# A hybrid encoder layer on one core: idle products on other tiles, the order of the attention heads, and the last blocks of w_down row by row

## The chip, the cores and the metric

The kernel runs on one core of a Trainium2 chip. The metric is the device time of one execution in microseconds (us). The time of the kernel before is the median of its runs; one more execution was taken with the hardware profiler, and all rows of the profile come from it.

## The reference

One layer over 512 tokens of width 1024, all in float32. Two mixers in parallel (a state-space scan and a gated spatial mixer) are merged by gates, then come cross-attention to 256 memory tokens and a SwiGLU feed-forward net. What matters for this change is the part from w_out on:

```
h = h + merged @ w_out
q = rms_norm(h) @ w_q; k = memn @ w_k; v = memn @ w_v            # memn = rms_norm(mem), 256 x 1024
s = einsum('blhd,bmhd->bhlm', q, k) * 256 ** -0.5                # 4 heads of 256
o = einsum('bhlm,bmhd->blhd', softmax(s), v)
h = h + o @ w_xo
n = rms_norm(h)
h = h + (silu(n @ w_gate) * (n @ w_up)) @ w_down                 # 2816 wide
return rms_norm(h)
```

## The kernel before

**Three products for one.** Every float32 operand is split in two, a high part and a low one (`split`, L83: ScalarE casts the high part, VectorE subtracts it). A product of two operands is three matmuls, high by high, high by low, low by high (`mm3`, L393; `product`, L1231, has its own). A matmul has 128 rows, a stationary operand of 128 columns and a moving one of 256 or 512. In the profile the three engines are PE (with PEld for the stationary loads), DVE (VectorE) and ACT (ScalarE).

**Weights.** A plan lists all weight blocks in the order of their use. `next_w` (L366) takes the next one; it also starts loads of later blocks (3 ahead, up to 7 for special ones) and the split of those up to 2 ahead (L99). The raw blocks, high parts and low parts rotate through 3 buffers each (tags raw, hi and lo), so a block's split waits until the block three places before it was used to the end. For w_gate, w_up, w_q and w_down the products are of a form with 7 block products in place of 8 (blocks named 1 to 7), whose operands are sums of blocks; some sums are made by DMA in DRAM (dsum) ahead of time.

**Order.** The program is written as one long sequence, but the order on each engine is made by a planner, which runs a timing model and takes, of what its model has ready, the instruction that stands first in the program. Three things bind it: `tc.keep_in_program_order` (named `in_order`, L94) puts an instruction behind the one before it in the program on its engine; `tc.issue_after(ins)` puts what a block traces on that engine behind `ins`; and `later(n, fn)` (L483) traces `fn` at the first `tick` when enough products have been traced. PSUM has two pools: 5 banks ("mm", by `bank`) and 3 ("aux", by `aux`, L73 and L74).

**Operand offsets.** `APART = (48, 112)` (L116) are offsets, in elements, at which the high and low part of some tiles begin: hn, fn, and the sums of the block products. mn's high and low part both begin at 48. ot_hi and ot_lo begin at 0.

**The idle product.** `long_idle` (L551) is one product of 128 by 512 whose result nobody reads. It takes the first 128 columns of its tile as the stationary operand and 512 columns as the moving one. There are two: behind the transposes of the last row before the feed-forward net, on ot_hi (from `feat_norm(..., behind=ot_hi)`, L1630), and at L1787, inside the first of the ten units of w_gate and w_up, on fn_hi.

**From w_out to the units.** `tokm` (L436) makes a product by token rows: w_out in two halves of 512 columns. Each finished row of 128 tokens is added to h, normalized and turned by 8 transposes into feature layout (`to_feat`, L556, tile ptr). w_k (`feat`, L399, stationary w_k, moving mn, 256 columns) and w_v (`tokm`, stationary mn, moving w_v, 512 columns) follow, then w_q in block products, interleaved with the heads of the attention. `scores(hd)` (L1510) makes 24 score products and the softmax of a head (numbered 0 to 3 in the code), `turn_probs` (L1534) turns its probabilities by 8 transposes (tile ppt) and splits them (p_hi, p_lo), and `values` (L1545) makes 12 products (tile po) and splits them into ot. The order at the end of the attention:

```
    values(0, *pts.pop(0))
    probs2 = scores(2)
    turn(1, probs1)
    probs3 = scores(3)
    values(1, *pts.pop(1))
    later(0.2, lambda: turn(2, probs2, last_mm[0].ins))
```

Then w_xo (tile pt): the first half of its columns in four steps of two feature blocks, all four token rows in each step; the first step needs head 0 of ot only. The second half goes two token rows at a time. The rows are normalized and turned (`ptr`), and the gate and up products of the last columns (tile pf) and ten units (tiles px, pv, pq) follow.

**w_down.** `rows_product` (L1762) makes the products of one chunk of a block for given rows; a block has 6 chunks, of 2 feature blocks each and 1 in the last. `down_product` (L1773) runs over the chunks, both token rows (tiles dx[0] and dx[1], 128 by 512) in each. Block 7 goes onto dx; `onto_h` (L1867) subtracts dx from h on VectorE; block 4, the last, goes onto the same dx. At the end the last two chunks of block 4 are held back: dx[1] is added to h without them, row 2 (dx[0]) is finished with them, and the last row gets them as two products of 256 columns (tile pcut). `finish`, `finish_last` and `write` (L1840 to L1865) sum the squares (ACT), take the root (a power on GpSimd, POOL), scale (DVE and ACT) and write out.

Of the kernel before, what the change touches and what calls it, by code (L numbers as in the profile page):

```python
# [17 lines left out]
P = 128  # L18
D = 1024
T = 512  # L20
NT = T // P
KD = D // P
M = 256
NM = M // P
# [28 lines left out]
def hybrid_layer_kernel(  # L53
# [23 lines left out]
    def bank(name):  # L77
        return pm.tile([P, 512], F32, tag="mm", name=name)
# [314 lines left out]
    def mm3(ps, a, b, start, stop, free=False):  # L393

        for i, (x, y) in enumerate(((0, 0), (0, 1), (1, 0))):
            last_mm[0] = nc.tensor.matmul(ps, a[x], b[y], start=start and i == 0, stop=stop and i == 2,  # L396
                                          skip_group_check=free)
# [38 lines left out]
    def tokm(w, c0, act, nk, evac, ntok=NT, last=2, kpt=2, hook=None, cut=None, t0=0, behind=None, fine=False):  # L436

        toks = range(t0, t0 + ntok)
        ps = {t: bank(f"pt{t - t0}") for t in toks}
        nw = nk // kpt  # L440
        held = []
        full = slice(0, 512)
        for wi in range(nw):
            hi, lo = next_w(w, wi * kpt, kpt, c0, 512)
            held.append((wi, hi, lo))
            if hook is not None and wi == nw - last:
                hook()
            if wi < nw - last:
                todo, held = held, []
                for t in toks:  # L450
                    end = cut is not None and t == ntok - 1 and wi == nw - last - 1
                    tok_block(ps[t], t, todo, act, kpt, full, wi == 0, end)
                    if end:
                        cut(None, ps[t])
                    if fine:
                        tick(1.3)
                if not fine:
                    tick(1.3 * ntok)
        for t in toks:
            if cut is not None and t == ntok - 1:  # L460
                for i in range(2):
                    p = aux("pcut", (P, 256))
                    tok_block(p, t, held, act, kpt, slice(256 * i, 256 * i + 256), True, True)
                    cut(i, p)
            else:
                with nullcontext() if behind is None or t > t0 else tc.issue_after(behind):
                    tok_block(ps[t], t, held, act, kpt, full, nw == last, True)
                evac(t, ps[t])
            tick(1.3 * len(held))
# [13 lines left out]
    def later(n, fn):  # L483

        side["later"].append((side["now"] + n, fn))
# [62 lines left out]
        for i in range(2):  # L548
            nc.vector.scalar_tensor_tensor(dst[:, HALF[i]], src[:, HALF[i]], r, g[:, HALF[i]], ALU.mult, ALU.mult)

    def long_idle(x):  # L551

        p = aux("long")
        in_order(nc.tensor.matmul(p, x[:, 0, 0:P], x[:, 0, :], start=True, stop=True))

    def to_feat(src, hi, lo, tsl, full=None, skip=None, part=(0, 1), behind=None):  # L556

        for q in part:
            ps = aux("ptr", (P, 4, P))
            for j in range(4):  # L560
                k = 4 * q + j
                tr = nc.tensor.transpose(ps[:, j, :], src[:, k * P:(k + 1) * P], ident)  # L562
                row_tr[0] = tr.ins
                if behind is not None:
                    in_order(tr)
            if q != skip:
                turned[:] = split(hi[:, 4 * q:4 * q + 4, tsl], lo[:, 4 * q:4 * q + 4, tsl], ps)
            if full is not None:
                nc.scalar.copy(full[:, 4 * q:4 * q + 4, tsl], ps)
        if behind is not None:  # L570
            long_idle(behind)

    xsp = [None]

# [861 lines left out]
    def add_evac(half, layer, fin, fin0=None):  # L1436

        def f(t, ps):
            nc.vector.tensor_tensor(h[:, t, HALF[half]], h[:, t, HALF[half]], ps, ALU.add)
            sum_sq(hss[:, layer, t, half:half + 1], h[:, t, HALF[half]])  # L1440
            if half == 1:
                fin(t, hss[:, layer, t, :])
            elif fin0 is not None:
                fin0(t)
        return f

    def feat_norm(g, hi, lo, full=None, skip=False, behind=None):

        return lambda t, ss: norm_feat(h[:, t, :], g, hi, lo, slice(t * P, (t + 1) * P), ss, full,
                                       0 if skip and t >= 2 else None, behind if t == NT - 1 else None)  # L1450

    mg = (mg_hi, mg_lo)
    for half in range(2):
        tokm(w_out, half * 512, mg, KD, add_evac(half, 0, feat_norm(g_x, hn_hi, hn_lo, hfull, True)))


    mn = (mn_hi, mn_lo)
# [49 lines left out]
            qs[hd] = (qq[:, 0], qq[:, 1])  # L1507
        split(qs[hd][0][:, :, ts], qs[hd][1][:, :, ts], src)

    def scores(hd):  # L1510
        q_hi, q_lo = qs.pop(hd)
        scale = XD ** -0.5
        prob = ap_.tile([P, NT, M], F32, tag="prob", name="prob", bufs=1) if hd % 2 == 0 else \
            np_.tile([P, NT, M], F32, tag="gain", name="prob", bufs=2)
        for i in range(2):
            ps = bank("psc").rearrange("p (t m) -> p t m", t=2)
            for tt in range(2):
                t = 2 * i + tt
                tsl = slice(t * P, (t + 1) * P)
                for k in range(2):  # L1520
                    mm3(ps[:, tt, :], (q_hi[:, k, tsl], q_lo[:, k, tsl]),
                        (kt_hi[:, 2 * hd + k, :], kt_lo[:, 2 * hd + k, :]), k == 0, k == 1)
            mx, nm, sm, rs = (ap_.tile([P, 2], F32, tag=k, name=k, bufs=4) for k in ("mx", "nm", "sm", "rs"))
            nc.vector.tensor_reduce(mx, ps, AX.X, ALU.max)
            nc.vector.tensor_scalar(nm, mx, -scale, None, ALU.mult)
            for tt in range(2):
                nc.scalar.activation(prob[:, 2 * i + tt, :], ps[:, tt, :], AF.Exp, bias=nm[:, tt:tt + 1],
                                     scale=scale, accum_out=sm[:, tt:tt + 1])
            nc.vector.reciprocal(rs, sm)
            for tt in range(2):  # L1530
                nc.vector.tensor_scalar(prob[:, 2 * i + tt, :], prob[:, 2 * i + tt, :], rs[:, tt:tt + 1], None, ALU.mult)
        return prob

    def turn_probs(hd, prob, behind=None):  # L1534
        p_hi = ap_.tile([P, NM, T], F32R, tag="p_hi", name="p_hi", bufs=2)
        p_lo = ap_.tile([P, NM, T], F32R, tag="p_lo", name="p_lo", bufs=2)
        for mt in range(NM):
            ps = aux("ppt", (P, NT, P))
            with nullcontext() if behind is None else tc.issue_after(behind):
                for t in range(NT):  # L1540
                    nc.tensor.transpose(ps[:, t, :], prob[:, t, mt * P:(mt + 1) * P], ident)
            split(p_hi[:, mt, :], p_lo[:, mt, :], ps.rearrange("p t m -> p (t m)"))
        return p_hi, p_lo

    def values(hd, p_hi, p_lo):  # L1545
        for dt_ in range(2):
            ps = bank("po")
            cs = slice(hd * XD + dt_ * P, hd * XD + dt_ * P + P)
            for mt in range(NM):
                mm3(ps, (vts[0][:, mt, cs], vts[1][:, mt, cs]), (p_hi[:, mt, :], p_lo[:, mt, :]), mt == 0, mt == NM - 1)  # L1550
            split(ot_hi[:, 2 * hd + dt_, :], ot_lo[:, 2 * hd + dt_, :], ps)

    def query_product(ps, n, q, start=False):
# [51 lines left out]
    values(0, *pts.pop(0))  # L1605
    probs2 = scores(2)
    turn(1, probs1)
    probs3 = scores(3)
    values(1, *pts.pop(1))
    later(0.2, lambda: turn(2, probs2, last_mm[0].ins))  # L1610
    later(0.7, lambda: turn(3, probs3))
    later(1.2, lambda: values(2, *pts.pop(2)))
    later(1.7, lambda: values(3, *pts.pop(3)))
# [13 lines left out]
    full = fp.tile([P, KD, T], F32, tag="full", name="full", bufs=1)  # L1627


    fin = add_evac(1, 1, feat_norm(g_f, fn_hi, fn_lo, full, behind=ot_hi))  # L1630
    held = []
    for t0 in (0, 2):
        ps = {t: bank(f"pt{t - t0}") for t in (t0, t0 + 1)}
# [233 lines left out]
    def onto_h(ps, t0, half, op):  # L1867
        for t in range(2):
            hs = h[:, t0 + t, HALF[half]]
            nc.vector.tensor_tensor(hs, hs, ps[t], op)  # L1870

    dv = [bank(f"dv{t}") for t in range(2)]
    dq = [bank("dq0"), aux("dq1")]
    down_product(dx, 1, True, range(2, CHUNKS))
# [11 lines left out]
    onto_h(dq, 0, 0, ALU.add)  # L1886
    for t in range(2):
        finish(t)
    down_product(dx, 7, False)
    onto_h(dx, 2, 0, ALU.subtract)  # L1890
    for t in range(2, 4):
        first_half(t, 0)

    held = []
    for c in range(CHUNKS):
        ops_ = next_w(w_down, 4, c)
        if c < CHUNKS - 2:
            rows_product(dx, 4, c, ops_, (0, 1), slice(0, 512), False, c == CHUNKS - 3)
        else:
            held.append((c, ops_))  # L1900
    finish_last(None, dx[1])
    for c, ops_ in held:
        rows_product(dx, 4, c, ops_, (0,), slice(0, 512), False, c == CHUNKS - 1)
    nc.vector.tensor_tensor(h[:, 2, HALF[1]], h[:, 2, HALF[1]], dx[0], ALU.add)
    finish(2)
    for i in range(2):
        p = aux("pcut", (P, 256))
        for c, ops_ in held:
            rows_product({1: p}, 4, c, ops_, (1,), slice(256 * i, 256 * i + 256), c == CHUNKS - 2, c == CHUNKS - 1)
        finish_last(i, p)  # L1910
    tick()
    sx.close()
# [32 lines left out]
```

## Time and profile before

| | us |
|---|---|
| median of 3 runs | 872.29 (871.88 to 872.76) |
| the profiled execution | 871.72 |
| its span, first to last instruction | 869.9 |
| PE busy | 856.6 |
| DVE busy | 648.1 |
| ACT busy | 475.0 |
| POOL busy | 106.2 |

A row of the page's groups, of the timeline or of the chain names the engine, the line, the operation and out<-in by the program's tile names. Line 396 is `mm3`, line 1240 `product`, line 85 and 86 the two steps of `split`, line 562 the transposes of `to_feat`, line 1541 those of the probabilities, line 554 the idle product. In the timeline a row has the start, the duration, and in brackets the idle time of the engine before it and what ended that. Matmuls are pipelined: a matmul's duration is longer than the step to the next one. In the chain of waits a row has start, time and what ran, with the count.

### The profile page before, as it was taken

What the parts mean: (1) busy time and instruction counts of PE and PEld (TensorE: products, weight loads), DVE (VectorE), ACT (ScalarE), POOL (GpSimd) and SP (SyncE); (2) the same over time, 40 slices, a digit from 0 to 9 for tenths busy, and PEclk for the clock granted to TensorE, in tenths of its full rate; (3) what the DMA queues carried; (4) which work ended last, traced back from release to release, by engine and by line L of the source; (5) the groups of instructions that cost most, each with busy time, mean ns of one, the idle gap of its engine ahead of it and who ended that gap; (6) DMA issues with size and microseconds to landing.
All of it is one profiled execution on the core that took longest, in us unless ns stands there. A gap on an engine that the chain in (4) does not pass through costs nothing.

```text
span 869.9 us, 14841 instructions
## 1 busy us (share of the span) xinstructions
PE 856.6 (98%) x5893; PEld 762.3 (88%) x5893; DVE 648.1 (75%) x897; ACT 475.0 (55%) x704; POOL 106.2 (12%) x157
## 2 busy tenths in 40 slices
PE   8999999999999999999999999999999999999996
PEld 6788888888789988899899888999999999988875
DVE  5699588968748658679658646867877768899875
ACT  5544874276437534457557444645545455656663
POOL 1001155100611010110010001001111111000000
PEclk8999999999999999999999999999999999999998
DMA  7549279745639586945688153557798886577672
GB/s 244 153 127 258 72 210 237 169 123 170 158 95 246 142 241 197 284 105 167 206 256 219 50 166 98 145 134 179 173 239 207 209 211 153 134 211 226 198 244 89
DMA packets 110119, 155.40 MB, mean 179 GB/s; under 512 B 8969, under 2 KB 77089, under 8 KB 109986
## 3 DMA queue, kind: packets, MB, share of 16 engines
q1 hardware_dynamic: 91746, 128.27, 46.1%
q0 software_dynamic: 18016, 25.66, 18.6%
q8 instruction: 46, 0.75, 0.4%
q10 hardware_dynamic: 288, 0.52, 0.2%
q14 instruction: 23, 0.19, 0.1%
HBM read 148.70 MB, written 37.20 MB: 214 GB/s over the span
## 4 chain that ended last, share of the span: by engine, by line
PE 94%; ACT 2%; DMA 2%; DVE 1%; issue 1%; SPq 0%; POOL 0%; POOLq 0%; ACTq 0%; DVEq 0%
PE pf L396 25%; PE pt L396 18%; PE px L1240 13%; PE dx L396 7%; PE pq L1240 6%; PE dq L396 3%; PE pv L1240 3%; PE gx L1240 3%; PE qx L1240 3%; PE dv L396 2%; PE po L396 1%; PE gq L1240 1%; PE qq L1240 1%; PE py L1033 1%; PE ptr L562 1%; PE psc L396 1%
## 5 line engine op out<-in xcount | busy, mean ns | idle before, releaser
L85 ACT CAST whi<-wraw 128x1024 fp32r<-128x1024 f32 (+1 forms) x133 | 136.9, 1029 | 141.5 <-PE pf L396 42.1
L86 DVE TENSOR_TENSOR wlo<-wraw,whi 128x1024 fp32r<-128x1024 f32 (+1 forms) x133 | 158.6, 1194 | 71.5 <-ACT whi L85 70.2
L396 PE MATMUL pf<-xn,whi 128*128 128x512 f32 x320 | 99.8, 392 | 0.0
L1240 PE MATMUL px<-fn,whi 128*128 128x256 f32 x480 | 83.3, 276 | 0.0
L1240 PEld LDWEIGHTS px<-fn,whi 128*128 128x128 f32 x480 | 72.5, 188 | 0.2
L86 DVE TENSOR_TENSOR wlo<-b,whi 128x1024 fp32r<-128x1024 f32 x40 | 48.9, 1223 | 29.4 <-ACT whi L85 29.4
L396 PEld LDWEIGHTS pf<-xn,whi 128*128 128x128 f32 x320 | 59.6, 188 | 12.5 <-issue 0.5
L85 ACT CAST whi<-b 128x1024 fp32r<-128x1024 f32 x40 | 42.1, 1053 | 51.9 <-PE px L1240 28.5
L1240 PE MATMUL px<-fn,wlo 128*128 128x256 f32 x240 | 66.4, 277 | 0.0
L396 PE MATMUL pf<-xn,wlo 128*128 128x512 f32 x160 | 62.9, 393 | 0.0
L1240 PE MATMUL pq<-s,whi 128*128 128x256 f32 x320 | 55.1, 276 | 0.0
L396 PE MATMUL dx<-whi,s 128*128 128x512 f32 x170 | 53.5, 391 | 0.4 <-DVE h L1870 0.4
L86 DVE TENSOR_TENSOR wlo<-t,whi 128x1024 fp32r<-128x1024 f32 x30 | 36.7, 1224 | 19.9 <-ACT whi L85 19.9
L85 ACT CAST whi<-t 128x1024 fp32r<-128x1024 f32 x30 | 31.6, 1054 | 35.8 <-PE pv L1240 12.6
L1240 PEld LDWEIGHTS pq<-s,whi 128*128 128x128 f32 x320 | 48.2, 188 | 0.0
L1240 PEld LDWEIGHTS px<-fn,wlo 128*128 128x128 f32 x240 | 45.1, 188 | 0.0
L1240 PE MATMUL pq<-s,wlo 128*128 128x256 f32 x160 | 44.2, 277 | 0.0
L396 PE MATMUL pt<-whi,xn 128*128 128x512 f32 x128 | 43.7, 414 | 0.3 <-ACT xn L85 0.2
L396 PEld LDWEIGHTS dx<-whi,s 128*128 128x128 f32 x170 | 31.8, 188 | 7.4 <-issue 0.8
L312 POOL DMA_DIRECT2D dsum<-in_w_down_dram x12 | 13.3, 1109 | 191.5 <-DMA dsum<-in_w_down_dram 191.5
L396 PEld LDWEIGHTS pf<-xn,wlo 128*128 128x128 f32 x160 | 30.1, 188 | 6.3 <-issue 0.2
L396 PE MATMUL dx<-wlo,s 128*128 128x512 f32 x85 | 33.1, 391 | 0.0
(480 smaller groups left out, 2333.6 us busy)
## 6 DMA issues: line engine op xcount, KB each, us to landing
wraw<-in_w_in_dram SPq DMA_DIRECT2D x35, 512.0 KB, 5.5
dsum<-in_w_down_dram SPq DMA_DIRECT2D x20, 512.0 KB, 5.8
wraw<-dsum SPq DMA_DIRECT2D x20, 512.0 KB, 3.9
b<-in_w_gate_dram SPq DMA_DIRECT2D x15, 512.0 KB, 4.2
b<-in_w_up_dram SPq DMA_DIRECT2D x15, 512.0 KB, 5.8
wraw<-in_w_down_dram SPq DMA_DIRECT2D x15, 512.0 KB, 5.0
dsum<-in_w_down_dram POOLq DMA_DIRECT2D x10, 512.0 KB, 8.0
dsum<-dsum POOLq DMA_DIRECT2D x10, 512.0 KB, 6.0
```

The lines of the kernel that those rows point to most:

```text
L85: hi = nc.scalar.copy(dst_hi, src)
L86: lo = nc.vector.tensor_tensor(dst_lo, src, dst_hi.bitcast(F32), ALU.subtract)
L312: plan[j + step][1].append((0, lambda d=dst, x=more: nc.gpsimd.dma_start(d, x, accum_op=ALU.add)))
L396: last_mm[0] = nc.tensor.matmul(ps, a[x], b[y], start=start and i == 0, stop=stop and i == 2, skip_group_check=free)
L562: tr = nc.tensor.transpose(ps[:, j, :], src[:, k * P:(k + 1) * P], ident)
L1033: in_order(nc.tensor.matmul(ps[64 * j:64 * j + 64, :], a, b, start=g % 4 == k == 0, stop=k == 2, tile_position=(0, 64 * j), skip_group_che ...
L1240: nc.tensor.matmul(ps[:, j, :], a[x], b[y], start=start and j == k == i == 0, stop=k == 3 and i == 2, skip_group_check=True)
```

## The change

Three parts, and no change to what is computed.

1. The idle product takes a choice of feature blocks and tokens. The one before the units reads fn_hi (feature blocks 0 and 1, tokens 0 to 255) and not ot_hi. A new one is made behind the transposes of w_out's last row; it reads mn_hi, feature blocks 0 and 1, all 256 columns. Those 8 transposes become kept in program order, as the ones before the units are already.
2. In the attention the scores of head 3 are issued behind the last transpose of head 1's probabilities. The values of head 1 are traced after the first rows of w_xo's first step and issued behind the first four transposes of head 2's probabilities.
3. In w_down the last two chunks of block 7 and the first two of block 4 are done row by row: both chunks for tile 0, then both for tile 1. The products of the last row's last two chunks are issued behind the last product of row 2.

```
-    def long_idle(x):
+    def long_idle(x, ks=slice(0, 1), ts=slice(0, T)):
         p = aux("long")
-        in_order(nc.tensor.matmul(p, x[:, 0, 0:P], x[:, 0, :], start=True, stop=True))
+        in_order(nc.tensor.matmul(p.rearrange("p (k t) -> p k t", k=ks.stop), x[:, 0, 0:P], x[:, ks, ts],
+                                  start=True, stop=True))
...
-            long_idle(behind)
+            long_idle(*behind)
...
     for half in range(2):
-        tokm(w_out, half * 512, mg, KD, add_evac(half, 0, feat_norm(g_x, hn_hi, hn_lo, hfull, True)))
+        tokm(w_out, half * 512, mg, KD, add_evac(half, 0, feat_norm(g_x, hn_hi, hn_lo, hfull, True, behind=(mn_hi, slice(0, 2), slice(0, M)))))
...
+    ends = []
+
-    def scores(hd):
+    def scores(hd, behind=None):
...
-                    mm3(ps[:, tt, :], ...)
+                    with nullcontext() if behind is None else tc.issue_after(behind):
+                        mm3(ps[:, tt, :], ...)
...
                 for t in range(NT):
-                    nc.tensor.transpose(ps[:, t, :], prob[:, t, mt * P:(mt + 1) * P], ident)
+                    tr = nc.tensor.transpose(ps[:, t, :], prob[:, t, mt * P:(mt + 1) * P], ident)
+            ends.append(tr.ins)
...
-    def values(hd, p_hi, p_lo):
+    def values(hd, p_hi, p_lo, behind=None):
...
-                mm3(ps, (vts[0][:, mt, cs], vts[1][:, mt, cs]), (p_hi[:, mt, :], p_lo[:, mt, :]), mt == 0, mt == NM - 1)
+                with nullcontext() if behind is None else tc.issue_after(behind):
+                    mm3(ps, (vts[0][:, mt, cs], vts[1][:, mt, cs]), (p_hi[:, mt, :], p_lo[:, mt, :]), mt == 0, mt == NM - 1)
...
-    probs3 = scores(3)
-    values(1, *pts.pop(1))
+    probs3 = scores(3, ends[-1])
     later(0.2, lambda: turn(2, probs2, last_mm[0].ins))
+    later(0.2, lambda: values(1, *pts.pop(1), behind=ends[-2]))
...
-    fin = add_evac(1, 1, feat_norm(g_f, fn_hi, fn_lo, full, behind=ot_hi))
+    fin = add_evac(1, 1, feat_norm(g_f, fn_hi, fn_lo, full, behind=(fn_hi, slice(0, 2), T0)))
...
+    def row_by_row(q, c0):
+        pair_ = [(c, next_w(w_down, q, c)) for c in (c0, c0 + 1)]
+        for t in range(2):
+            for c, ops_ in pair_:
+                rows_product(dx, q, c, ops_, (t,), slice(0, 512), False, c == CHUNKS - 1)
...
-    down_product(dx, 7, False)
+    down_product(dx, 7, False, range(CHUNKS - 2))
+    row_by_row(7, CHUNKS - 2)
     onto_h(dx, 2, 0, ALU.subtract)
...
-    for c in range(CHUNKS):
+    row_by_row(4, 0)
+    for c in range(2, CHUNKS):
...
     nc.vector.tensor_tensor(h[:, 2, HALF[1]], h[:, 2, HALF[1]], dx[0], ALU.add)
+    row2 = last_mm[0].ins
     finish(2)
     for i in range(2):
         p = aux("pcut", (P, 256))
         for c, ops_ in held:
-            rows_product({1: p}, 4, c, ops_, (1,), slice(256 * i, 256 * i + 256), c == CHUNKS - 2, c == CHUNKS - 1)
+            with tc.issue_after(row2):
+                rows_product({1: p}, 4, c, ops_, (1,), slice(256 * i, 256 * i + 256), c == CHUNKS - 2, c == CHUNKS - 1)
         finish_last(i, p)
```

The prediction counts heads from 1: its head 2 is `hd` 1 in the code, its head 4 `hd` 3.

More of the change, by code (lines that the diff above doesn't have):

```diff
@@ L1520, in scores @@
                 for k in range(2):
-                    mm3(ps[:, tt, :], (q_hi[:, k, tsl], q_lo[:, k, tsl]),
-                        (kt_hi[:, 2 * hd + k, :], kt_lo[:, 2 * hd + k, :]), k == 0, k == 1)
+                    with nullcontext() if behind is None else tc.issue_after(behind):
+                        mm3(ps[:, tt, :], (q_hi[:, k, tsl], q_lo[:, k, tsl]),
+                            (kt_hi[:, 2 * hd + k, :], kt_lo[:, 2 * hd + k, :]), k == 0, k == 1)
             mx, nm, sm, rs = (ap_.tile([P, 2], F32, tag=k, name=k, bufs=4) for k in ("mx", "nm", "sm", "rs"))
```

## The prediction

> **What bounds the kernel now.** I read the page first, then the chain of waits, then who waited on TensorE, then the timelines at the places that the diff touches.
>
> ```profile
> span 869.9 us, 14841 instructions
> PE 856.6 (98%) x5893; PEld 762.3 (88%) x5893; DVE 648.1 (75%) x897; ACT 475.0 (55%) x704; POOL 106.2 (12%) x157
> PE 94%; ACT 2%; DMA 2%; DVE 1%; issue 1%; SPq 0%; POOL 0%; POOLq 0%; ACTq 0%; DVEq 0%
> ```
>
> TensorE is busy for all but 13.3 us (869.9 - 856.6) and is 94% of the chain. So time can come from three sources only: idle gaps of TensorE, the tail behind its last product, and the rate at which products follow each other. Of the gaps, the view of waits on TensorE names two that the diff touches:
>
> ```profile
> PE po L396 <- ACT p_hi L85: 1.1, 1, 1.1
> PE dx L396 <- DVE h L1870: 0.4, 1, 0.4
> ```
>
> The rate is less plain. In the chain of waits a row gives start, time and count, so time over count is the step from product to product:
>
> ```profile
> 396.72 10.96 PE pf L396 x93
> 407.68 22.40 PE pt L396 x96
> ...
> 554.03 16.96 PE pf L396 x144
> 570.99 2.83 PE pq L1240 x24
> 574.05 8.18 PE px L1240 x72
> ...
> 593.11 8.16 PE px L1240 x72
> ...
> 816.81 14.96 PE dq L396 x66
> ```
>
> A product over 256 columns takes 117.8 ns a step in w_k (10.96/93) and from 554 to 573 us (16.96/144, 2.83/24), but 113.3 from 593 on (8.16/72). One over 512 columns takes 233.3 in w_v (22.40/96) and 226.7 in w_down (14.96/66). It isn't the throttle: in the view by stretches (span, then busy and count of PE, PEld, DVE, ACT, POOL, granted clock, DMA) the clock is full (1.00) where the step is long:
>
> ```profile
> 560.00:570.00 10.00, 10.00 (x87) 10.00 (x86) 6.72 (x6) 4.33 (x5) 0.00 (x0) 1.00 0.01 2
> ```
>
> So there is a long and a short step at one clock, and a stretch keeps the one that it has. What switches it I read from the two idle products of the trace (TensorE's timeline):
>
> ```profile
> 551.52 0.39 PE L554 MATMUL long<-ot_hi 128*128 128x512 f32 x1
> 551.75 0.40 PE L1240 MATMUL pv<-fn,whi 128*128 128x256 f32 x2
> ...
> 552.10 0.40 PE L1240 MATMUL pv<-fn,whi 128*128 128x256 f32 x2
> 573.65 0.40 PE L554 MATMUL long<-fn 128*128 128x512 f32 x1
> 573.89 0.40 PE L1240 MATMUL px<-s,whi 128*128 128x256 f32 x2
> ...
> 574.24 0.39 PE L1240 MATMUL px<-s,whi 128*128 128x256 f32 x2
> ...
> 574.58 0.39 PE L1240 MATMUL px<-s,whi 128*128 128x256 f32 x2
> ```
>
> The one on ot_hi took 0.23 us (551.52 to 551.75), and three products behind it still take 0.35 us (551.75 to 552.10, 117 ns each). The one on fn took 0.24 us, and three products soon behind it take 0.34 (574.24 to 574.58, 113 ns). The operand seems to decide: ot_hi begins at offset 0 of its tile, fn_hi at 48 (APART, L116).
>
> **The change part by part**, against the profiled execution's own 871.72 us (span 869.9 and 1.8 around it); the median of the runs shown is 872.29, 0.57 more.
>
> (a) The idle product before the units reads fn_hi (k blocks 0 and 1, tokens 0 to 255) in place of ot_hi. The count stays one, +0.01 us by 0.24 against 0.23. If it switches as the one at 573.65 did, the products between 551.75 and 573.65 run short: 18 of pv, 144 of pf and 24 of pq, 186 by 4.5 ns, 0.84 us. Bounds: -0.83 us, and 0. I take -0.8, because operand tile and offset are those of the product that switched.
>
> (b) A new idle product behind the last transposes of w_out's fourth row reads mn_hi, which begins at 48 too. It costs 0.24 us and nothing hides it, since TensorE has no gap there. The transposes become pinned in order; they are in that order already. It needs a PSUM bank of the small pool, and w_k's products are queued behind it; the one at 551.52 came late enough to wait for none. If it comes as late behind them as the one at 551.52, it leaves some 80 of w_k's 93 products to be shortened: 80 by 4.5 ns is 0.36. Bounds: +0.24 (no switch), and -0.8 if w_v's 96 products follow as well (96 by 6.6 ns, 0.63 more). w_v has mn as the stationary operand, though, and never leaves 233.3, so I leave it out: -0.1.
>
> (c) Attention. These are the rows of TensorE, DVE and ACT:
>
> ```profile
> 477.13 0.60 PE L1541 MATMUL ppt<-ident,prob 128*128 128x128 f32 x4
> 477.48 0.37 PE L396 MATMUL psc<-kt_hi,qq 128*128 128x256 f32 x1
> ...
> 483.03 0.60 PE L1541 MATMUL ppt<-ident,prob 128*128 128x128 f32 x4
> 484.75 0.73 PE L396 MATMUL po<-p_hi,vt 128*128 128x512 f32 x2 [1.11 <-ACT p_hi L85]
> 481.18 0.61 DVE L1531 TENSOR_SCALAR prob<-prob,rs 128x256 f32<-128x256 f32 x2
> 484.08 1.10 ACT L85 CAST p_hi<-ppt 128x512 fp32r<-128x512 f32 x2
> ```
>
> Head 2's first four transposes stand at 477.13, then the 48 score products of heads 3 and 4 (477.48 to 483.03), then the other four. The values of head 2 follow at once and wait 1.11 us for ACT's p_hi. The diff puts head 4's 24 scores behind those four transposes and the values behind w_xo's first products. Then 2.7 us of scores and the first w_xo products lie between transposes and values, more than p_hi needs (483.03 to 485.18): the 1.11 us go. No product is added, nor a DMA. What is late next: the pinned transposes themselves. Their probabilities are scaled by 481.79 (481.18 + 0.61), while head 3's scores end at 480.2 (477.48 + 24 by 113.3 ns). The scores of head 4 and everything behind would stand for 1.6 us, unless the planner puts w_xo's first products (ready: head 1's ot_lo is done by 479.55, below) in between. In the old order it left these transposes behind all the scores of head 4, though they come first in the program; so its own model had them ready no earlier than there, and in the new order it will fill some 2.7 us. I take -1.1. Bounds: -1.2, and +0.5 (1.6 of wait for 1.1).
>
> ```profile
> 478.27 1.28 DVE L86 TENSOR_TENSOR ot_lo<-po,ot_hi 128x512 fp32r<-128x512 f32 x2
> ```
>
> The Trainium skill, TensorE: Matmul & The Clock Gate, section "Part 3: Packing small matmuls — row/col tiling", says that matmuls run strictly in order and only weight loads are pulled ahead. It speaks against the pin; by it alone, without filling, this part would give +0.5. The trace agrees so far: no product passed the 1.11 us wait.
>
> (d) The joint of w_down's blocks 7 and 4:
>
> ```profile
> 846.34 0.39 PE L396 MATMUL dx<-whi,s 128*128 128x512 f32 x1
> 847.15 0.47 PE L396 MATMUL dx<-whi,s 128*128 128x512 f32 x1 [0.42 <-DVE h L1870]
> ...
> 848.39 0.63 PE L396 MATMUL dx<-whi,s 128*128 128x512 f32 x2
> 848.92 0.50 PE L396 MATMUL dx<-wlo,s 128*128 128x512 f32 x1
> 849.25 0.62 PE L396 MATMUL dx<-whi,s 128*128 128x512 f32 x2
> 844.92 1.22 DVE L86 TENSOR_TENSOR s<-a_low,s 128x1024 fp32r<-128x1024 f32 x1
> 846.32 0.69 DVE L1870 TENSOR_TENSOR h<-h,dx 128x512 f32<-128x512 f32 x1 [0.18 <-PE dx L396]
> 847.64 1.22 DVE L86 TENSOR_TENSOR wlo<-wraw,whi 128x1024 fp32r<-128x1024 f32 x1 [0.63 <-ACT whi L85]
> 846.56 1.05 ACT L85 CAST whi<-wraw 128x1024 fp32r<-128x1024 f32 x1 [1.86 <-DMA wraw<-dsum]
> ```
>
> 846.34 to 847.15 is 0.81 us for a step of 0.227, so 0.58 are lost, and 0.18 more behind it: 848.39 to 849.25 is 0.86 for three steps of 0.227, where the second weight chunk's wlo comes late. Row by row, tile 0 ends nine products earlier, 2.0 us, and DVE's subtraction of 0.69 fits beside tile 1's nine, before or behind the 1.22 us of s. What is late next: that wlo. Its cast waits for a DMA until 846.56, so it is done at 848.86 whatever PE does, while the second chunk's second product would come at 848.15. If it is kept waiting there, nothing is won (0.7 lost for 0.8); if tile 1's products of the first chunk are put in between, all 0.8 are. Neither is in the trace; between 0 and -0.8 I take the middle, -0.4. The weight tile of block 7's fifth chunk is held three products (0.7 us) longer, which the same DMA covers.
>
> (e) The end row. Seven half products of the last tile stand before tile 2's last product; behind the pin they come after it, so tile 2 is done 0.8 us sooner (7 by 0.115) while TensorE's end stays. The tail is longer than it must be:
>
> ```profile
> 863.36 0.55 POOL L1837 TENSOR_TENSOR r<-ms,mhalf 128x1 f32<-128x1 f32 x1 [25.28 <-DVE ms L1822]
> 864.09 1.02 POOL L1837 TENSOR_TENSOR r<-ms,mhalf 128x1 f32<-128x1 f32 x1 [0.17 <-DVE ms L1822]
> 863.95 0.75 DVE L1864 SCALAR_TENSOR_TENSOR h<-h,r,g_o 128x512 f32<-128x512 f32 x1
> ```
>
> GpSimd's power takes 0.55 us alone and 1.02 beside DVE's scaling of tile 2. With that scaling 0.8 us sooner, the last power is alone: -0.45. Against it, ACT's scaling of tile 2 may slip ahead of the last tile's row sum: +0.15. I take -0.3. The Trainium skill, SBUF — State Buffer, section "Who interferes with whom", has a DVE instruction with two SBUF inputs block a GpSimd one that reads SBUF; by it the gain is the 0.47 of the two rows, and by a power that varies of itself it is 0.
>
> Sum: -0.8 - 0.1 - 1.1 - 0.4 - 0.3 = -2.7 us: 869.0 by this execution, **869.6 us** by the median. Its own range is 868.6 to 870.5.
>
> **The rivals.**
> 1. The idle products don't switch the step: (a) gives 0, (b) +0.24, the sum -1.6, **870.7 us**. For it: one of two seen did not. Against it: that one read another tile. By the Trainium skill, TensorE: Matmul & The Clock Gate, section "Back-to-back issue gap", a warm step depends on the column count alone, and an idle product could only cost; this rival is what it would give, but the two steps at clock 1.00 speak against it.
> 2. A wait takes the place of the one removed: the pinned transposes stand for their probabilities, and PSUM banks taken by w_xo's products hold head 4's scores up as well. (c) gives +0.5 to +1.4, the time is **871.2 to 872.1 us**. For it: 481.79 against 480.2. Against it: the planner's own old order.
> 3. The other side. From 574.05 to 748.14, where dx begins, 1536 products run at 113.3 (174.09 us). An idle product reads fn_hi just before them; today it meets the long step and leaves the short one. If (a) works, it meets the short step, and might leave the long one: 1536 by 4.5 ns, +6.9 us, **876.5**. It decides as soon as the stretch is long for over a third (2.3 us): then the kernel is no faster than before, and with half of it about 873. For it: no trace shows such a product meeting the short step. Against it: 1536 products with their waits never fell out of it.
>
> ```profile
> 748.14 3.31 PE dx L396 x14
> ```
>
> That the change doesn't do what it says is in (d): the wait only moves to wlo; it is inside the forecast's range.
>
> **How the numbers follow.** Forecast 0.52, rival 1 0.15, rival 2 0.15, rival 3 or another long stretch at the slow step 0.18. About 0.2% (1.7 us) is what a measurement of this kernel can tell from no change. Faster by more (under 870.5): the forecast and the low side of rival 1, 0.54. Within: rivals 1 and 2, 0.26. Slower (over 874.0): 0.20, rival 3 and its like. The range runs from 868.2 (the good ends of (b) and (d)) to 875.0, which takes in rivals 1 and 2 and half of rival 3's way.
>
> **What would show it.** (a) Steps of 113 ns from 551.8 to 573 and after 574. (b) An idle product behind the transposes in w_k and 113 ns after it; w_v unchanged at 233. (c) No row of po waiting for p_hi, w_xo products before head 4's scores, and no wait of ppt over 0.3 us. (d) No wait for h at the joint and tile 1's products ahead of the second chunk's. (e) Both powers near 0.55 us. The forecast is wrong if the units run at 117.8, or if ppt waits 1.5 us.

## The result and the profile after

The kernel after takes 869.43 us (median of 7 runs, 868.60 to 871.38), the kernel before 872.29 (7 runs, 871.07 to 873.61); the ratio is 0.9968, 95% interval 0.9957 to 0.9979, so 2.8 us less (1.8 to 3.8). The profiled execution took 870.48 us. Its page, first two rows:

```profile
span 868.7 us, 14845 instructions
...
PE 855.1 (98%) x5894; PEld 760.1 (88%) x5894; DVE 648.3 (75%) x897; ACT 474.8 (55%) x704; POOL 106.0 (12%) x157
```

TensorE is still busy for all but 13.6 us. Who it waited for (the view of waits on TensorE: total, times, longest):

```profile
PE ppt L1545 <- DVE prob L1535: 1.1, 1, 1.1
...
PE dv L396 <- DVE wlo L86: 0.5, 1, 0.5
...
PE dx L396 <- DVE h L1876: 0.4, 1, 0.4
```

The wait of po for p_hi is gone and one of ppt for its probabilities, equally long, has come. The wait at the joint is there as before. The chain of waits (start, time, what) shows the steps and the stages:

```profile
396.12 0.83 PE pf L396 x7
397.18 9.75 PE pf L396 x86
406.93 21.97 PE pt L396 x96
428.90 2.75 PE qx L1241 x24
...
546.24 1.59 PE pf L396 x14
...
552.88 16.32 PE pf L396 x144
...
760.28 8.61 PE dx L396 x38
...
784.78 7.41 DMA wraw<-in_w_down_dram
...
816.25 14.96 PE dq L396 x66
```

w_k now runs at 113.4 ns (9.75/86), w_v at 228.9 (21.97/96), the stretch before the units at 113.3 (16.32/144). Three more rows of the chain of before cut its time at the same places:

```profile
430.08 2.74 PE qx L1240 x24
...
547.33 1.59 PE pf L396 x14
...
762.21 8.61 PE dx L396 x38
```

The starts of these rows (w_k, qx, pf x14, dx x38, dq x66) and the span, which is printed to 0.1 us, give six stages. Every kernel's chain has these rows; in e6_joint_pin and e11_fill the dx row counts 36. Within a stage, executions of the same instructions agree to about 0.1 us: the attention stage takes 117.23 to 117.34 in the six kernels with part 2 as it is, the stretch to w_down 214.04 to 214.17 in the nine in which the idle product before the units reads from 48. The first and the fifth stage vary more, from 395.3 to 399.4 and from 54.4 to 56.0 with the same instructions, and have transfers in their chains. So the other four are compared.

| us | to w_k | w_k, w_v | attention, w_xo | to w_down | w_down, first | to the end |
|---|---|---|---|---|---|---|
| before | 396.72 | 33.36 | 117.25 | 214.88 | 54.60 | 53.09 |
| after | 396.12 | 32.78 | 117.34 | 214.04 | 55.97 | 52.45 |
| e1_idle | 397.76 | 32.78 | 117.24 | 214.08 | 54.40 | 53.04 |
| e2_attn | 396.01 | 33.35 | 117.31 | 214.90 | 54.40 | 53.03 |
| e3_down | 396.37 | 33.35 | 117.25 | 214.89 | 55.60 | 52.44 |
| e4_no_attn | 399.40 | 32.78 | 117.25 | 214.08 | 54.40 | 52.49 |
| e5_dve_order | 398.85 | 32.78 | 116.67 | 214.17 | 54.45 | 52.48 |
| e6_joint_pin | 396.70 | 32.78 | 117.34 | 214.10 | 55.92 | 51.66 |
| e7_tail | 396.62 | 32.78 | 117.33 | 214.08 | 54.40 | 52.19 |
| e8_operand | 395.25 | 33.60 | 117.23 | 214.88 | 54.40 | 52.44 |
| e9_offset | 395.61 | 32.80 | 117.24 | 214.10 | 54.40 | 52.45 |
| e10_all | 396.67 | 32.78 | 116.59 | 214.10 | 54.40 | 51.56 |
| e11_fill | 399.03 | 32.79 | 115.92 | 214.12 | 55.50 | 51.54 |

From before to after: -0.58, +0.09, -0.84 and -0.64, together -1.97 us; the +0.09 of attention is no more than the stage varies by itself. The sum lies inside the interval of the timed runs (1.8 to 3.8), though below its middle; the fifth stage took 1.4 us more in after's profiled execution, for weights that landed late (the DMA row at 784.78 and the wait of dv).

**The idle products** (TensorE's timeline: start, time, instruction):

```profile
550.43 0.40 PE L554 MATMUL long<-fn 128*128 128x512 f32 x1
...
551.02 0.39 PE L1241 MATMUL pv<-fn,whi 128*128 128x256 f32 x2
...
551.36 0.39 PE L1241 MATMUL pv<-fn,whi 128*128 128x256 f32 x2
...
571.76 0.40 PE L554 MATMUL long<-fn 128*128 128x512 f32 x1
...
572.35 0.39 PE L1241 MATMUL px<-s,whi 128*128 128x256 f32 x2
...
572.69 0.39 PE L1241 MATMUL px<-s,whi 128*128 128x256 f32 x2
```

Soon behind the first, three products take 0.34 us (551.02 to 551.36), the short step. The second now meets the short step and leaves it short (572.35 to 572.69, 0.34).

**Attention** (timelines of TensorE, DVE and ACT):

```profile
479.02 0.28 PE L396 MATMUL psc<-kt_hi,qq 128*128 128x256 f32 x1
480.41 0.70 PE L1545 MATMUL ppt<-ident,prob 128*128 128x128 f32 x4 [1.11 <-DVE prob L1535]
...
477.10 1.28 DVE L86 TENSOR_TENSOR ot_lo<-po,ot_hi 128x512 fp32r<-128x512 f32 x2
...
479.34 0.69 DVE L1528 TENSOR_REDUCE mx<-psc 128x2 f32<-128x512 f32 x1 [0.28 <-PE psc L396]
...
480.01 0.61 DVE L1535 TENSOR_SCALAR prob<-prob,rs 128x256 f32<-128x256 f32 x2
...
477.46 0.21 ACT L1531 ACTIVATION_READ_ACCUMULATOR prob<-psc,nm 128x1 f32 x1
```

ACT has the sums at 477.67. DVE first makes two ot_lo and two maxima, the second of which waits for head 3's last score, and scales at 480.01. The transposes stand directly behind that last score (479.02): the scaling they need lies behind an instruction that waits for the product just ahead of them.

**The joint and the tail** (DVE, TensorE; then GpSimd, ACT and its DMA issue), and two rows of before:

```profile
844.36 1.22 DVE L86 TENSOR_TENSOR s<-a_low,s 128x1024 fp32r<-128x1024 f32 x1
845.76 1.29 DVE L1876 TENSOR_TENSOR h<-h,dx 128x512 f32<-128x512 f32 x2 [0.18 <-PE dx L396]
...
846.59 0.47 PE L396 MATMUL dx<-whi,s 128*128 128x512 f32 x1 [0.42 <-DVE h L1876]
...
861.66 0.28 PE L396 MATMUL pcut<-whi,s 128*128 128x256 f32 x1
...
861.61 0.55 POOL L1843 TENSOR_TENSOR r<-ms,mhalf 128x1 f32<-128x1 f32 x1 [24.08 <-DVE ms L1828]
863.58 0.55 POOL L1843 TENSOR_TENSOR r<-ms,mhalf 128x1 f32<-128x1 f32 x1 [1.43 <-DVE ms L1828]
...
862.19 0.72 ACT L1868 ACTIVATE rest<-rest,r 128x512 f32<-128x512 f32 x1 [0.26 <-POOL r L1843]
862.82 0.40 ACT L523 ACTIVATE sq<-h 128x256 f32<-128x256 f32 x1
...
864.95 0.37 ACTq L1871 DMA_DIRECT2D out_dram<-h  x1
```

```profile
862.48 0.28 PE L396 MATMUL pcut<-whi,s 128*128 128x256 f32 x1
...
865.92 0.37 ACTq L1865 DMA_DIRECT2D out_dram<-h  x1
```

Both subtractions at the joint stand behind s and come as late as before. In the tail both powers take 0.55 us, but ACT's scaling of tile 2 (862.19) stands ahead of the last row sum (862.82).

### The profile page after: what moved, and what is told of

The parts are those of the page before. It is cut to its first block, busy times and chain, and to the rows that moved or that the text cites. A ratio compares the mean times of both kernels' runs of the same rounds, so it can differ in the third digit from the quotient of the medians.

```text
span 868.7 us, 14845 instructions
## 1 busy us (share of the span) xinstructions
PE 855.1 (98%) x5894; PEld 760.1 (88%) x5894; DVE 648.3 (75%) x897; ACT 474.8 (55%) x704; POOL 106.0 (12%) x157
## 4 chain that ended last, share of the span: by engine, by line
PE 91%; DMA 3%; ACT 2%; DVE 2%; issue 1%; SPq 0%; POOL 0%; POOLq 0%; ACTq 0%; DVEq 0%
PE pf L396 25%; PE pt L396 18%; PE px L1241 13%; PE dx L396 7%; PE pq L1241 6%; PE pv L1241 3%; PE gx L1241 3%; PE qx L1241 3%; PE dq L396 2%; PE gq L1241 1%; PE psc L396 1%; PE po L396 1%; PE qq L1241 1%; PE py L1034 1%; PE ptr L563 1%
```

## The experiments

### The three parts alone, and the first and third together

e1_idle is the kernel before with part 1 alone:

```
+    def long_idle(x, ks=slice(0, 1), ts=slice(0, T)):
...
+ behind=(mn_hi, slice(0, 2), slice(0, M))    # w_out's fourth row
+ behind=(fn_hi, slice(0, 2), T0)             # ahead of the units
```

> The kernel before with the two idle products of the change alone (one on mn_hi behind w_out's last transposes, the one before the units on fn_hi). My theory, from the trace of after: the step of the products behind them is what changes, 0.77 us between 551 and 573 us, 0.12 in w_k and 0.44 in w_v, so 1.3 us faster than before (871.0 by the median of 872.29), with steps of 113 ns before the units and below 233 ns in w_v. Rival: the steps are chance of one execution and the time stays within 0.3 us of before.

Measured: 870.94 us, ratio 0.9989 (0.9976 to 1.0002). The interval of the timed runs just takes in no change; the stages decide: -0.58 and -0.80, 1.4 us, as expected, and the others that are compared are untouched.

e2_attn is part 2 alone:

```
-    probs3 = scores(3)
-    values(1, *pts.pop(1))
+    probs3 = scores(3, ends[-1])
+    later(0.2, lambda: values(1, *pts.pop(1), behind=ends[-2]))
```

> The kernel before with the attention part alone. My theory: the wait only moves, from the values of head 2 for p_hi (1.1 us) to its pinned transposes for their probabilities (1.1 us), so between 0.1 us faster and 0.3 us slower than before. Rival (the forecast's own step): 1.1 us faster, since something else of after's trace hid the gain.

Measured: 872.39 us, ratio 0.9996 (0.9982 to 1.0010); the stage takes 117.31 us for 117.25. The wait moved and nothing was won (timeline of TensorE):

```profile
480.86 0.70 PE L1544 MATMUL ppt<-ident,prob 128*128 128x128 f32 x4 [1.11 <-DVE prob L1534]
```

e3_down is part 3 alone:

```
+    down_product(dx, 7, False, range(CHUNKS - 2))
+    row_by_row(7, CHUNKS - 2)
...
+    row_by_row(4, 0)
...
+            with tc.issue_after(row2):
```

> The kernel before with the w_down part alone (joint and end row). My theory, from the trace of after: the wait of 0.42 us at the joint stays, since block 7's last products stand in the mixed order after all; 0.26 us come from block 4 and 0.15 from the tail: 0.4 us faster. Rival (the forecast's terms): 0.7 us faster, with the wait for h gone.

Measured: 871.23 us, ratio 0.9989 (0.9979 to 0.9999). The last stage is 0.65 us shorter, so more than my 0.4: I had left out that the last transfer lands sooner (below). But the wait for h is there (waits on TensorE), so the rival's reason is wrong:

```profile
PE dx L396 <- DVE h L1870: 0.4, 1, 0.4
```

e4_no_attn is after without part 2:

```
-    probs3 = scores(3, ends[-1])
-    later(0.2, lambda: values(1, *pts.pop(1), behind=ends[-2]))
+    probs3 = scores(3)
+    values(1, *pts.pop(1))
```

> The kernel after without its attention part (idle products and w_down only). If the attention part is worth nothing, the time is that of after, 869.4 +- 0.3 us, and the sum of the first and third part is the whole gain (1.3 + 0.4 by the traces, 2.9 by the medians: then some 1.2 us of the medians are still without a place). Rival: the attention part is worth its 1.1 us, and this kernel takes 870.5.

Measured: 869.68 us, ratio 0.9969 (0.9957 to 0.9980): the time of after. The attention part is worth nothing here, and the three parts add up without touching each other's stages.

### Where the idle product's operand begins

e8_operand changes only what the two idle products read:

```
-behind=(fn_hi, slice(0, 2), T0)
+behind=(ot_hi, slice(0, 2), T0)
-behind=(mn_hi, slice(0, 2), slice(0, M))
+behind=(mn_hi, 16)        # flat: 512 elements from 16 on
```

> The kernel after with two idle products changed. The one before the units reads ot_hi (blocks 0 and 1, tokens 0 to 255: the shape of the change, the tile of before). The one in w_k reads mn_hi as one run of 512 elements that begins 16 further on, at 64 from the tile's start and not 48. If where the operand begins decides, as the forecast has it, the units' first 186 products take 117.8 ns again (0.77 us back); if the shape of two blocks of 256 decides, they keep 113.3. In w_k: 113 ns if any operand away from the tile's start does it, 117.8 if 48 is needed. Rival: any idle product at that place switches the step, whatever it reads.

Measured (869.62 us, one run): both fall back. Chain of waits:

```profile
396.32 10.13 PE pf L396 x86
406.45 22.40 PE pt L396 x96
...
552.78 16.96 PE pf L396 x144
```

117.8 ns (10.13/86, 16.96/144) and 233.3 (22.40/96). The stage w_k, w_v takes 33.60 us, 0.24 over before: the price of an idle product that switches nothing. The shape of two blocks doesn't do it, nor does mn_hi from 64 on. The rival, that any idle product there switches, is refuted.

e9_offset has the same edit with other beginnings, both flat:

```
-behind=(ot_hi, slice(0, 2), T0)
+behind=(ot_hi, 48)
-behind=(mn_hi, 16)
+behind=(mn_hi, 8)
```

> The kernel after with other operands of the two idle products: before the units ot_hi again, but as one run of 512 elements from 48 on (stationary operand still from 0); in w_k mn_hi from 8 on, which is 56 from the tile's start. If the beginning of the moving operand decides, not the tile, the units' first 186 products take 113.3 ns (207.3 us for this stretch becomes 206.5), though it is ot_hi that is read; if the tile or the stationary operand decides, 117.8. For 56: the stages w_k and w_v take 46.8 us if any beginning that is no multiple of 64 elements does it, 47.6 if only 48 does.

Measured (868.39 us, one run): both switch, though one reads ot_hi.

```profile
396.68 9.77 PE pf L396 x86
406.44 21.97 PE pt L396 x96
...
552.29 16.32 PE pf L396 x144
```

The stretch from the first product on fn to dx takes 206.5 us (207.3 in e8_operand). The kernel before reads ot_hi in one run of 512 elements too, with the same stationary operand; only the moving operand's beginning differs: from 0 no switch, from 48 a switch. For mn_hi, 64 no, 56 and 48 yes.

These beginnings are counted from the tile's start. In the programs as built the tiles themselves don't start at a multiple of 256 bytes, which is 64 elements, but 64 bytes behind one (ot_hi at 104256, mn_hi at 158016, fn at 70976). By address, then, the operands that switch begin 0 bytes (48 elements) or 32 bytes (56) behind a multiple of 256, and those that don't begin 64 bytes behind one (0 and 64). Four beginnings give no rule, neither "off the multiples of 64 elements" nor "on a multiple of 256 bytes"; others weren't tried.

### Attention

e5_dve_order is after, with DVE's order turned:

```
+        scaled.append(done.ins)          # the last scaling of a head
...
+    with tc.issue_after(scaled[1]):
+        values(0, *pts.pop(0))
+        probs2 = scores(2)
```

> The kernel after, with DVE's splits of head 1's output (ot_lo, 1.28 us) and the maxima of head 3's scores queued behind the scaling of head 2's probabilities. My theory: in after the pinned transposes stand 1.1 us because DVE, which has the exponentials' sums at 477.7 us, does two ot_lo and two maxima first and scales only at 480.0; with the order turned the probabilities are done before head 3's last score, the wait of ppt is under 0.2 us, and the stage from the first query product to the end of w_xo is 1.0 to 1.2 us shorter (117.34 in after, 117.25 in before). Rival: the wait moves once more, to the values or to w_xo's first products, which need ot_lo, and the stage stays within 0.3 us.

Measured (871.16 us, one run): the stage takes 116.67 us, 0.67 less than in after. The pinned transposes wait no more, but those of head 3 do (timeline of TensorE): eight take 1.47 us, four of head 2 took 0.60.

```profile
481.87 0.60 PE L1546 MATMUL ppt<-ident,prob 128*128 128x128 f32 x4
...
486.75 1.47 PE L1546 MATMUL ppt<-ident,prob 128*128 128x128 f32 x8
```

So DVE's order was the cause of the wait in after, and about half of what it cost is lost again one head later: theory and rival each hold in part.

### The joint and the tail

e6_joint_pin is after with a pin in `row_by_row`, for block 7 (`pin` is true there):

```
         for t in range(2):
+            with tc.issue_after(last_mm[0].ins) if pin and t else nullcontext():
```

> The kernel after, with tile 1's products of block 7's last two chunks queued behind tile 0's by a pin. My theory: in after the planner put these products back in the mixed order (tile 0's last one stands fourth from the end), so that the wait of 0.42 us for h could not go; with the pin tile 0 is done 9 products, 2.0 us, before the end, DVE's subtraction goes ahead of s, and the wait goes: 0.6 us from the stretch that begins with the last step of block 7 (18.41 us from the subtraction's start to the last scaling in after). Rival of the forecast: the wait only moves to the second chunk's wlo, whose weights land late, and the stretch stays within 0.2 us.

Measured (870.31 us, one run): the last stage takes 51.66 us, some 0.8 less than in after. DVE's timeline:

```profile
844.95 0.68 DVE L1876 TENSOR_TENSOR h<-h,dx 128x512 f32<-128x512 f32 x1
845.54 1.22 DVE L86 TENSOR_TENSOR s<-a_low,s 128x1024 fp32r<-128x1024 f32 x1
```

The subtraction now stands ahead of s and waits for nothing; the gap of 0.58 us (0.81 from product to product in after too, less a step of 0.227) is gone. What the planner had done shows in the program as built, TensorE's last products of block 7 in after (dx0 is tile 0, dx1 tile 1; the chunks' weights are 8650 and 8668):

```
dx0<-whi_8668
dx1<-whi_8650
dx1<-whi_8668
dx0<-wlo_8669
dx0<-whi_8668
dx1<-wlo_8669
dx1<-whi_8668
```

e7_tail is after with ACT's scaling of tile 2 behind the last row sum:

```
+            with tc.issue_after(sq):
+                write(2, r2[0])
             write(t, inv_root(NT, ss[:, 0:1]))
```

> The kernel after, with ACT's scaling of tile 2 queued behind the last tile's second row sum. My theory: of the 0.45 us that the shorter power gives in the tail, after gives back 0.3, because ACT's scaling of tile 2 (0.72 us) stands ahead of that row sum; behind it, the time from the last pcut product to the last output transfer falls from 3.29 us to about 3.0 (3.44 in before). Rival: the power meets DVE's or ACT's scaling again and takes 1.0 us as in before, and the tail is 3.4 us.

Measured (869.20 us, one run): from the last pcut product to the last output's issue 3.03 us (860.62 to 863.65), the stage 0.26 shorter. ACT's and GpSimd's timelines: the row sum waits only for its input, and the power still takes 0.55.

```profile
861.50 0.42 ACT L523 ACTIVATE sq<-h 128x256 f32<-128x256 f32 x1 [0.62 <-DVE h L1857]
...
862.28 0.55 POOL L1844 TENSOR_TENSOR r<-ms,mhalf 128x1 f32<-128x1 f32 x1 [1.17 <-DVE ms L1829]
```

### All together, twice

e10_all has the three mendings, with two more pins on DVE:

```
+            with tc.issue_after(nms[-1]) if (hd, i) == (2, 1) else nullcontext():
+                nc.vector.tensor_reduce(mx, ps, AX.X, ALU.max)
...
+    with tc.issue_after(nms[5]):
+        turn(1, probs1)
+        probs3 = scores(3, ends[-1])
```

> The kernel after with the three mendings together: DVE's order in attention (as in the run with that order, and besides head 3's second maximum behind the first one's scaling, and p_lo and head 4's maxima behind head 3's), the pin at the joint, ACT's order in the tail. By the stages measured one by one: 0.6 us from attention (0.8 to 1.0 if the two short waits of head 3's transposes, 0.4 us, go with DVE's order), 0.7 from the joint, 0.25 from the tail: 1.6 to 1.9 us faster than after, 867.6 to 867.9 by its median of 869.4, and 4.5 under before. Rival: the shorter stages meet later weight transfers and the sum is under 1 us.

Measured: 868.42 us against 873.04 of before, ratio 0.9960 (0.9943 to 0.9976). The median lies above the expected 867.6 to 867.9, with a before that is 0.75 higher than the 872.29 they were reckoned from. By stages it is 1.6 us under after, the low end; attention won only 0.08 on top of e5_dve_order, and a wait of head 3's transposes stays (waits on TensorE):

```profile
PE ppt L1548 <- DVE prob L1537: 0.3, 1, 0.3
```

e11_fill keeps the joint and the tail so, leaves DVE alone and takes back the pin of head 4's scores: they stand ahead of head 2's last transposes again, as in before, and six products of w_xo are pinned between these transposes and head 2's values. That is not the forecast's order, in which w_xo's products come before head 4's scores, ahead of the pinned transposes; that one wasn't run.

```
-    probs3 = scores(3, ends[-1])
+    probs3 = scores(3)
-    later(0.2, lambda: values(1, *pts.pop(1), behind=ends[-2]))
+    later(0.2, lambda: values(1, *pts.pop(1), behind=last_mm[0].ins))
...
+ tokm(w_xo, ..., ahead=ends[-1])   # its first six products behind the transposes
```

> The kernel after with the pins at the joint and in the tail, and with attention in the order that the forecast had in mind: head 4's scores ahead of head 2's last transposes again, six products of w_xo pinned between these transposes and head 2's values. If the forecast's reason holds as a mechanism (the cover was only missing), neither the transposes nor the values wait, and attention with w_xo is 1.0 to 1.1 us shorter than before (119.8 us from the first query product to the last transposes becomes 118.8; 119.9 in after, 119.2 with DVE's order); then the kernel takes 867.3 to 867.6. Rival: p_hi, for which the values wait, comes from an ACT that has the exponentials of heads 3 and 4 ahead of it, so that part of the wait stays or moves to head 3's transposes, and the gain of this stretch is under 0.6 us.

Measured: 867.63 us against 871.91 of before, ratio 0.9946 (0.9923 to 0.9970); the lowest median here. Attention and w_xo take 115.92 us, 1.33 under before (118.6 by the expectation's own measure). The view of waits on TensorE names neither ppt nor po, so the rival is refuted. Its timeline, from head 4's last score on:

```profile
484.65 0.28 PE L396 MATMUL psc<-kt_hi,qq 128*128 128x256 f32 x1
484.77 0.60 PE L1547 MATMUL ppt<-ident,prob 128*128 128x128 f32 x4
485.13 0.48 PE L396 MATMUL pt<-whi,ot_hi 128*128 128x512 f32 x1
...
486.95 0.71 PE L396 MATMUL po<-p_hi,vt 128*128 128x512 f32 x2
```

By stages it is 2.2 us under after and 0.7 under e10_all; the intervals of the three ratios overlap.

## Why the prediction came out as it did

The forecast said 869.6 and 869.43 was measured, but its parts didn't all come true: by stages they sum to -1.97, not -2.7.

- **(a) Right**, in size and reason. -0.8 was forecast; the stage is 0.80 shorter in e1_idle, 0.84 in after. The moving operand's beginning decides: ot_hi from 0 gives the 0.8 back, ot_hi from 48 wins it. The Trainium skill, TensorE: Matmul & The Clock Gate, section "Back-to-back issue gap", has the warm step follow from the column count alone; here 256 columns took 113.3 and 117.8 ns in e9_offset and e8_operand at the same place, so the measurement differs.
- **(b) Mis-sized.** -0.1 was forecast, -0.58 came. w_k won 0.15, about as worked out (10.96 us in before, 10.81 from 396.12 to 406.93), and w_v 0.43 (22.40 to 21.97). The step that failed is "w_v has mn as the stationary operand, though, and never leaves 233.3, so I leave it out": behind a short w_k it runs at 228.9, between its two steps. The bound for no switch, +0.24, was met to the digit by e8_operand.
- **(c) Wrong.** -1.1 was forecast, +0.09 came, which can't be told from nothing. The step that failed is "so its own model had them ready no earlier than there, and in the new order it will fill some 2.7 us": the planner filled nothing and put the transposes directly behind head 3's last score, where they stood 1.11 us. This is rival 2's mechanism, at a lower price than its 0.5 to 1.4: the wait took 1.11 and not 1.6, as much as went for p_hi. The 1.6 had counted to the end of both scalings; in after the transposes begin at 480.41, before both are done at 480.62 (480.01 + 0.61). The row quoted for the rival was there: probabilities ready at 481.79 against a last score at 480.2. e5_dve_order shows that DVE's order made the transposes late. e11_fill shows that w_xo's products cover the wait for p_hi, as the forecast reckoned, and that this wins 1.33 without moving head 4's scores at all. Whether they would also have covered the pinned transposes, as the forecast's order has it, no run shows.
- **(d) Two thirds of the size, by another way.** -0.4 was forecast. From the dq row to the last pcut product before took 45.67 us, after 45.41: -0.26. "Row by row, tile 0 ends nine products earlier" didn't happen, as the order above shows: without a pin the planner put tile 0's last product third from the end, where it stood before. The wait for h stayed; what went is the second loss, the 0.18 for wlo, since tile 1's products of block 4 do stand in between. With the pin, e6_joint_pin shortened the same stretch by another 0.70, to 44.71 (816.84 to 861.55): 0.96 in all, more than the "all 0.8". Of the 0.70 the gap is 0.58, and the step behind it 0.09 (0.31 in after, 0.22 with the pin), which the forecast hadn't counted.
- **(e) Right in size, from more terms.** -0.3 was forecast; from the last product to the end of the span it is 7.42 before and 7.04 after, -0.38 (the terms that follow give -0.44; the spans are rounded to 0.1). The power fell from 1.02 to 0.55 as worked out, which agrees with the rule of the Trainium skill cited there; ACT's scaling did slip ahead, at 0.26 (what e7_tail got back) and not 0.15; and the span ends 3.75 us after the last output's issue and not 3.98, a term the forecast lacked.
- **Rival 1** fell with after's own steps of 113.3 and 113.4 ns (e8_operand shows what it would have been like), **rival 3** with the second idle product, which met the short step and left it short: the 1536 products kept 113.3.

So the total was met in good part by luck: (c) missed by 1.2 us and (d) by 0.14, while (b) and (e) gave 0.56 back. The stages then hold 1.97 of the 2.86 us between the medians. The other 0.9 has no place in them; the interval of the timed runs, which begins at 1.8, allows that it is nothing. e4_no_attn has the same: 2.8 by the medians, 2.0 by the stages.

Open: why the moving operand's beginning switches the step, and which beginnings do; why the planner did not fill ahead of the transposes, though head 1's last ot_lo was done at 478.38 (477.10 + 1.28) and the last score began at 479.02; whether the change itself makes late weights in the fifth stage more frequent (four of the ten kernels with its w_down part, mended or not, took 55.5 us or more there, the three without it 54.4 to 54.6; the chains of three of the four have weight transfers in this stage).

## What to carry to other kernels

A wait on the engine that bounds the kernel is worth its time only if other work is pinned into its place: an order that was written down without a pin was undone by the planner here (block 7), and a pin without filling moved the wait to an earlier product. Filling the wait where it stood (e11_fill) won more than reordering the products around it. Before moving a consumer forward, look up its producer's place in the producer's own queue, here a scaling behind a maximum that waited for the very product in front. Stage times cut at rows of the chain resolve some 0.1 us where the total of an execution varies by 2 to 3.

## What the runs showed of the hardware that was not expected

- An idle product switches the step of those behind it, from 117.8 to 113.3 ns for 256 columns, if its moving operand begins 48 or 56 elements into the tile, and not from 0 or 64 (0 or 32 bytes behind a multiple of 256 by address, and not 64). It costs 0.24 us.
- Products of 512 columns behind it ran at 228.9 ns, between 226.7 and 233.3: the switch is not all or nothing there.
- From the issue of the last output to the end of the span it took 3.98 us in before, where tile 2's two outputs were issued at 864.69 and 865.12, just ahead of the last tile's (SyncE's timeline), and 3.75 in after, where they were issued at 862.94 and 863.37. The view of DMA from 860 to 872 us has the four transfers without a break in before (355 to 403 GB/s in its full slices), and with one between tile 2's and the last tile's in after. That the transfers share a path is argued from this, not tried by itself.
